# A split-fp32 hybrid trunk on one core: inverse root on ScalarE with a Newton step, x for the value sums on the weights' queue, and a new spread of the block sums

## The chip, the cores and the metric

The kernel runs on one core of one Trainium2 chip. Its time is device microseconds from launch to end; a profile is one further execution of the same program, recorded by the hardware profiler. Engines are named as in the profile: PE (TensorE), with its weight loads as PEld; DVE (VectorE); ACT (ScalarE); POOL (GpSimd); SP (SyncE, here only an issuer of DMAs). "L1704" is line 1704 of the kernel file. Line numbers are those of the kernel before, unless it is said that they belong to the changed one, where the same line stands up to 14 further down.

## The reference

One decoder layer over 512 tokens of width 1024, in fp32:

```
proj  = x @ w_in            # q, k, v of three token mixers, and three gates
o_da  = differential attention (4 heads, two softmax maps, per-head RMSNorm)
o_sb  = stick-breaking attention (8 heads)
o_dl  = dilated windows (3 head groups x 4 heads, outputs of a slot merged
        by their softmax denominators)
m     = (sum_i sigmoid(gate_i) * (o_i @ w_branch_i)) @ w_out
x     = layer_norm(ALPHA * x + m)
x     = layer_norm(ALPHA * x + relu(x @ w_up)**2 @ w_down + gated embedding of p)
```

The per-head RMSNorm of the differential branch is `o * rsqrt(mean(o*o) + eps)`: this is the inverse root that the change computes in another way.

## The kernel before, in words

**Splits.** Every large product is done in three: each fp32 operand is split into a high and a low part, and PE multiplies high with high, high with low, low with high. Weights come in chunks of 128 x 1024 fp32 (512 KB). SP loads a chunk (`fill`, L163 to 186) into a ring of seven; `split_next` (L198 to 219) issues its high part as a cast on ACT (L212, "wh") and its low part as a subtraction on DVE (L214, "wl"), both into rings of six. A cast can run only when PE is done with the tile six chunks back.

**The main stream.** The work is a list of items, each a bank of PSUM filled by a run of matmuls (`mm`) and emptied by an evacuation (`ev`). The main loop (behind L1890) walks the items; between them `step()` advances generators for the attention heads (`sb_head`, `dil_head`, `da_block`) and the forms of x (`value_forms`, `mixer_forms`). A `yield` in a generator says "go on at the next step". So the Python order is an interleaving; a scheduler then fixes each engine's own order when the program is built, and each engine runs its list in that order.

**Seven products and the sums they need.** Many matrix products are done as 2 x 2 blocks with seven products instead of eight. That takes sums of weight blocks and sums of x blocks.
- *Weight sums* are made in DRAM by DMAs that POOL issues: copies (L1046) and accumulating DMAs (L1044), in the order of `sum_steps` (L1017 to 1070). Each has a dependency on `lows[0]`, the weight split four back, so that they spread over the stream. How many go out is a credit: each item adds `size * rate` (L1941 to 1948), and each whole unit issues one step. Late in the kernel the credit is 0.58 an item.
- *x sums for the value projection* (`value_forms`, L343 to 393): eight tiles xr of 128 x 512 fp32 (256 KB each, L347) come by POOL's queue; DVE combines them (L370, L363, L388, tile "fr"), and ACT and DVE split the results (L237 and L238, "u7", "u6", "u4", "u5"). `value_pair` (L395 to 443) uses them for two of the three dilated value groups; its items copy partial results by ACT (L427, L431) and merge them on DVE (L430 to 441, "dl_v"). `load_xr` (L324 to 336, L331) loads x a second time, later, for the gates.

**Around the change in time.** First PE finishes projections of q and k (L87 to 89, evacuated at L285 and L287, "dl_q", "dl_k"). Then the items of `value_pair` (L420 to 422) run, and dilated head 0 beside them: its scores (L1737, L1753 on PE), row maxima on DVE (L1740, L1761), exponentials on ACT (L1746, L1768), the exchange of row statistics between the strided orders by two small matmuls (L1778 with r of L1771, L1780 with r of L1774), a chain of small operations (L1784 to L1800, one exponential on ACT at L1795), the scaling of the tiles (L1802 and L1806 on DVE), transposes on PE (L1821, L1830) and the product with the values (L1842, L1847). Head 0 waits six extra yields ahead of its transposes (L1809).

**The differential branch.** `da_block` (L1649 to 1718) does one head and one quarter of the queries. After the fourth quarter of a head it takes four means of squares "ms" (128 x 4): L1703 on DVE makes mean plus eps, L1704 on POOL raises it to the power -0.5, L1705 on DVE multiplies by the softmax denominators' inverses. On DVE, L1705 holds up what stands behind it. On POOL, L1704 stands among the DMA issues of the weight sums, and an issue waits until one of the eight earlier transfers with its semaphore has landed. Sigmoids of the gates (L501) are issued after the last exponential (`last_exp`), so that ACT changes its function table once.

**The engines' queues.** SP: chunk loads. POOL: weight sums, both loads of x, a few shuffles, L1704.

Of the kernel before, what the change touches and what calls it, by code (L numbers as in the profile page):

```python
# [55 lines left out]
def trunk(tc, a, out):  # L56
    nc = tc.nc
    es = ExitStack()
    with es:
# [76 lines left out]
        ORDERED, AHEAD = 17, 4  # L136
        loads, chunks, placed = [], [], []
        lows = deque(maxlen=4)
        st = {"dma": 0, "split": 0}

        def load(src, w, own=False):
# [56 lines left out]
        def split_next():  # L198
            c = chunks[st["split"]]
            w, off = c["w"], c.get("off", 0)  # L200
            if c.get("pre"):
                c["pre"]()
            if c.get("dst") is None:
                h = ring.tile([P, 1024], F32R, name=nm("wh"), tag="wh", bufs=RING)
                lo = ring.tile([P, 1024], F32R, name=nm("wl"), tag="wl", bufs=RING)
                parts = [(h[:, :w], lo[:, :w], 0, w)]
                c["h"], c["l"] = parts[0][:2]
            else:
                parts = c["dst"]
            for h, lo, a0, a1 in parts:  # L210
                raw = c["from"]["raw"][:, off + a0:off + a1]
                i = nc.scalar.copy(h, raw)  # L212
                st["cast"] = getattr(i, "ins", i)
                i = nc.vector.tensor_sub(lo, raw, h.bitcast(F32))  # L214
                st["low"] = getattr(i, "ins", i)
                lows.append(st["low"])
            for t in (c["from"], *c.get("also", ())):
                t["uses"] -= 1
            st["split"] += 1
# [104 lines left out]
        def load_xr():  # L324

            r = {}
            for h in range(2):
                for th in range(2):
                    for kp in range(2):
                        t = slot("xr")  # L330
                        i = nc.gpsimd.dma_start(t.rearrange("p (k t) -> p k t", k=2),  # L331
                                                xt[:, 4 * h + 2 * kp:4 * h + 2 * kp + 2, 256 * th:256 * th + 256])
                        tc.add_manual_dep(getattr(i, "ins", i), lows[-1].name, mybir.DependencyInfo(
                            mybir.DependencyClass.Sync, mybir.DependencyReason.DATA), reason="not ahead of time")
                        r[h, th, kp] = t
            return [[r[h, th, kp] for kp in range(2)] for h in range(2) for th in range(2)]
# [6 lines left out]
        def value_forms():  # L343

            xr = [slot("xr") for _ in range(8)]
            for k, t in enumerate(xr):
                i = nc.gpsimd.dma_start(t, xt[:, k, :])  # L347
                tc.add_manual_dep(getattr(i, "ins", i), lows[-1].name, mybir.DependencyInfo(
                    mybir.DependencyClass.Sync, mybir.DependencyReason.DATA), reason="not ahead of time")

            def blk(kh, k, th):
                return xr[4 * kh + k].rearrange("p (t c) -> p c t", c=4)[:, 2 * th:2 * th + 2, :]

            def new():
                ts = [slot("fr") for _ in range(2)]
                return ts, [ts[k // 2].rearrange("p (k c t) -> p k c t", k=2, c=2)[:, k % 2] for k in range(4)]

            def parts(p, ts):
                form(vf, p, ts)
                vf[p] = [[(h[:, r * P:r * P + P], lo[:, r * P:r * P + P]) for r in range(2)] for h, lo in vf[p]]  # L360

            def neg_sub(o, i, j):
                nc.vector.scalar_tensor_tensor(o, i, -1.0, j, op0=OP.mult, op1=OP.subtract)  # L363

            for _ in range(WAIT):
                yield
            f7, o7 = new()
            with tc.issue_after(st["low"]):
                for k in range(4):
                    nc.vector.tensor_sub(o7[k], blk(1, k, 1), blk(0, k, 1))  # L370
            parts(7, f7)
            yield
            f6, o6 = new()
            with tc.issue_after(st["low"]):
                for k in range(4):
                    neg_sub(o6[k], o7[k], blk(0, k, 0))
            yield
            parts(6, f6)
            yield
            f4, o4 = new()  # L380
            for k in range(4):
                neg_sub(o4[k], o6[k], blk(1, k, 0))
            yield
            parts(4, f4)
            yield
            f1, o1 = new()
            for k in range(4):
                nc.vector.tensor_sub(o1[k], blk(0, k, 0), blk(0, k, 1))  # L388
            yield
            parts(5, f1)  # L390
            yield
# [53 lines left out]
        def v_items(nv, name, g):  # L445
            cs = [chunk(a["wv"][nv, c].rearrange("p k n -> p (k n)"), 1024) for c in range(4)]
            for tt in range(4):
                def mm(ps, tt=tt):
                    for k in range(8):
                        c = cs[k // 2]  # L450
                        s = slice((k % 2) * 512, (k % 2) * 512 + 512)
                        x1, x2 = xh[k][:, tt * P:tt * P + P], xl[k][:, tt * P:tt * P + P]
                        nc.tensor.matmul(ps, x1, c["h"][:, s], start=k == 0, stop=False)
                        nc.tensor.matmul(ps, x1, c["l"][:, s], start=False, stop=False)
                        nc.tensor.matmul(ps, x2, c["h"][:, s], start=False, stop=k == 7)
                        if k == 3:
                            yield

                def ev(ps, tt=tt):
                    if name == "sb_v":  # L460
                        v = [slot(name, F32R).rearrange("p (h two d) -> p h two d", two=2, d=64) for _ in range(2)]
                        pv = ps.rearrange("p (h d) -> p h d", d=64)
                        for i in range(2):
                            hs = slice(4 * i, 4 * i + 4)
                            nc.scalar.copy(v[i][:, :, 0, :], pv[:, hs, :])
                            nc.vector.tensor_sub(v[i][:, :, 1, :], pv[:, hs, :], v[i][:, :, 0, :].bitcast(F32))
                        V[name, g, tt] = v
                    else:
                        t = slot(name)
                        cp(t, ps)  # L470
                        V[name, g, tt] = t
                item(cs if tt == 3 else [], mm, ev, need=cs)
                items[-1]["rate"] = 1.4

        nt, nv = 2, 0
        order = main_order()
# [62 lines left out]
        def seven(forms, operand, bank_of, done):  # L539

            cs = {}
            for p in (2, 1, 7, 6, 4, 5, 3):
                for r in range(2):
# [19 lines left out]
                    if p == 5:  # L563
                        bank_of.get("sums", set()).add(len(items))
                    item(cs[p] if r else [], mm, ev, need=cs[p], bank=bank, size=0.5)
                    items[-1]["rate"] = 1.2

        msum = [[[dram.tile([P, 1024], F32, name=f"msum{n}_{m}_{i}") for i in range(4)] for m in range(2)]
                for n in range(3)]
# [67 lines left out]
        def branch_items(i):  # L637
            for half in range(2):
                cs = [chunk(a["wb"][i - 1, half, c].rearrange("p k n -> p (k n)"), 1024) for c in range(2)]
                for tt in range(4):  # L640
# [20 lines left out]
                    def pre(tt=tt, half=half):  # L661
                        sg[i, tt, half] = gate_sig(i, tt, half)
                    item(cs if tt == 3 else [], mm, ev, need=cs, bank=None if i == 1 else at_bank, size=0.5)
                    items[-1]["rate"] = 1.5
                    if i != 1:
                        items[-1]["pre"] = pre

# [30 lines left out]
        def branch_seven(i, behind):  # L698

            s, b, cs = {}, {}, {}  # L700
            for p in (2, 1, 7, 6, 4, 5, 3):
                for r in range(2):
# [31 lines left out]
                        m = merged[to]  # L734
                        (nc.vector.tensor_add if p in (1, 3) else nc.vector.tensor_sub)(m, m, g)
                    item([cs[p]] if r else [], mm, ev, need=[cs[p]], bank=bank, size=0.25)
                    items[-1]["rate"] = 1.5
                    to = {2: (r, 0), 7: (r, 1), 6: (2 + r, 1), 4: (2 + r, 0)}.get(p)
                    if to:
                        def pre(to=to):  # L740
# [19 lines left out]
            item([], mm, ev, size=0.08)  # L760

        last_plain = len(items)
        for it in items:
            it.setdefault("rate", 2.6)
        def first_gate(tt, half):
            g = gate_sig(1, tt, half)
            nc.vector.tensor_mul(merged[tt, half], merged[tt, half], g)
# [249 lines left out]
        def sum_steps():  # L1017
# [24 lines left out]
            def issue(o, i, plus):  # L1042
                if plus:
                    i = nc.gpsimd.dma_start(o, i, accum_op=OP.add, max_dma_last_dim=4096)  # L1044
                else:
                    i = nc.gpsimd.dma_start(o, i, max_dma_last_dim=4096)  # L1046

                tc.add_manual_dep(getattr(i, "ins", i), lows[0].name, mybir.DependencyInfo(
                    mybir.DependencyClass.Sync, mybir.DependencyReason.DATA), reason="spread over the main stream")

            w = a["wv"].rearrange("g c p k n -> g c p (k n)")
# [597 lines left out]
        def da_block(hd, qb):  # L1649
# [50 lines left out]
            if da_left[hd] == 0:  # L1700
                yield

                nc.vector.tensor_scalar(ss, ss, 1.0 / P, EPS, op0=OP.mult, op1=OP.add)  # L1703
                nc.gpsimd.tensor_tensor(ss, ss, mhalf.to_broadcast([P, 4]), OP.pow)  # L1704
                nc.vector.tensor_mul(ss, ss, da_rr[hd])  # L1705
                yield
                on = slot("on")
                nc.vector.tensor_mul(on.rearrange("p (b d) -> p b d", b=4), po.rearrange("p (b d) -> p b d", b=4),
                                     ss.unsqueeze(2).to_broadcast([P, 4, P]))
# [11 lines left out]
        def dil_head(hd):  # L1721
            while any(("dl_q", 4 * g + hd) not in T or ("dl_k", 4 * g + hd) not in T for g in range(3)):
                yield

            while hd == 1 and ("dl_v", 1, 3) not in V:
                yield
            q = [T["dl_q", 4 * g + hd] for g in range(3)]
            k = [T["dl_k", 4 * g + hd] for g in range(3)]
# [77 lines left out]
                nc.vector.tensor_scalar(o, o, mxx[:, c:c + 1], None, op0=OP.mult)  # L1806
            yield

            for _ in range(6 if hd == 0 else 0):  # L1809
                yield  # L1810

            src0 = {}
# [89 lines left out]
        for n, it in enumerate(items):  # L1902
# [39 lines left out]
            if 12 <= n < wout_at + 8:  # L1942
                credit += it["size"] * it.get("rate", 1.0)
            elif n > ple_at + 6:
                credit += 0.58
            while credit >= 1:
                credit -= 1
                next(sum_steps_, None)
# [142 lines left out]
```

## Time and profile before

| | us |
|---|---|
| median of 3 runs (lowest to highest) | 1063.72 (1063.63 to 1065.58) |
| the profiled execution | 1063.71 |
| span recorded in it | 1061.8 |
| PE busy / DVE / ACT / POOL in the span | 1039.9 / 773.6 / 589.7 / 182.1 |
| PE idle in the span | 21.9 |
| mean granted clock of PE | 0.991 |

The span is what the profiler saw between the first and the last instruction; 1.9 us of the execution lie around it. In the timelines a row is: start in us, length in us, engine, line, operation, result <- operands, how many, and in brackets how long the engine had been idle and what released it. In the rows of waits the numbers are: us in total, times, the longest. In the groups by line they are: busy us, mean ns of one, idle ahead of them. A matmul's length contains its pipeline, so two neighbours overlap; their distance is the cost. The granted clock is 1.00 when PE may run at full rate.

### The profile page before, as it was taken

How to read it: one execution, taken by the hardware profiler on the slowest of the kernel's cores; microseconds unless marked ns; L12 is line 12 of the kernel's file. 1: busy time of each engine (PE TensorE's matmuls, PEld its weight loads, DVE VectorE, ACT ScalarE, POOL GpSimd, SP SyncE). 2: the span in 40 equal slices, each digit the busy share in tenths (PEclk: the TensorE clock that was granted, in tenths of full speed). 3: DMA queues.
4: the chain of work that ended last, by engine and by line, in shares of the span. 5: the costliest groups of instructions: out<-in, count | busy, mean ns of one | idle time of the engine just before them, and what ended most of it. 6: DMA issues, size and time to landing. Idle time of an engine off the chain costs nothing.

```text
span 1061.8 us, 15061 instructions
## 1 busy us (share of the span) xinstructions
PE 1039.9 (98%) x5462; PEld 884.9 (83%) x5462; DVE 773.6 (73%) x1376; ACT 589.7 (56%) x1002; POOL 182.1 (17%) x279
## 2 busy tenths in 40 slices
PE   9999999998999998999999999999999999999996
PEld 6887788887888886788888888888999989989885
DVE  6887667639864743878766785889677877877966
ACT  6665545526444642667662663685665665666651
POOL 0003303220202312201111122111211111111000
PEclk9999999999999998999999999999999999999998
DMA  8358957995847999637999999179999999999512
GB/s 317 111 169 252 244 160 224 306 280 172 254 133 205 305 284 262 231 103 236 295 295 279 317 311 302 64 254 291 331 333 342 305 275 306 316 284 336 194 38 80
DMA packets 74346, 260.09 MB, mean 245 GB/s; under 512 B 9144, under 2 KB 10056, under 8 KB 74272
## 3 DMA queue, kind: packets, MB, share of 16 engines
q0 software_dynamic: 33616, 120.40, 43.3%
q1 hardware_dynamic: 40080, 137.81, 36.0%
q8 instruction: 43, 0.70, 0.3%
q10 hardware_dynamic: 576, 0.92, 0.2%
q14 instruction: 31, 0.25, 0.1%
HBM read 256.98 MB, written 111.17 MB: 347 GB/s over the span
## 4 chain that ended last, share of the span: by engine, by line
PE 81%; DMA 11%; issue 4%; DVE 2%; ACT 1%; POOL 0%; SPq 0%; DVEq 0%; POOLq 0%; ACTq 0%
PE mm L87 8%; PE mm L88 7%; PE mm L89 7%; DMA msum<-in_wgm_dram 4%; PE at L1207 4%; PE at L1208 4%; PE at L1209 4%; DMA bsum<-bsum 3%; PE at L554 3%; PE at L556 3%; PE at L555 3%; DMA gsum<-in_wg_dram 1%; PE at L89 1%; PE at L88 1%; PE at L87 1%
## 5 line engine op out<-in xcount | busy, mean ns | idle before, releaser
L214 DVE TENSOR_TENSOR wl<-raw,wh 128x1024 fp32r<-128x1024 f32 x254 | 308.9, 1222 | 124.6 <-ACT wh L212 122.4
L212 ACT CAST wh<-raw 128x1024 fp32r<-128x1024 f32 x254 | 265.9, 1050 | 234.6 <-PE mm L88 129.5
L87 PE MATMUL mm<-xhT,wh 128*128 128x512 f32 x304 | 122.6, 403 | 0.0
L89 PE MATMUL mm<-xhT,wl 128*128 128x512 f32 x304 | 120.2, 395 | 0.0
L88 PE MATMUL mm<-xlT,wh 128*128 128x512 f32 x304 | 120.1, 395 | 0.0
L1207 PE MATMUL at<-wh,hh 128*128 128x512 f32 x188 | 73.7, 392 | 0.0
L1208 PE MATMUL at<-wl,hh 128*128 128x512 f32 x188 | 73.7, 392 | 0.0
L87 PE MATMUL mm<-x1hT,wh 128*128 128x256 f32 x256 | 73.7, 288 | 0.0
L1209 PE MATMUL at<-wh,hl 128*128 128x512 f32 x188 | 73.1, 389 | 0.0
L88 PE MATMUL mm<-x1lT,wh 128*128 128x256 f32 x256 | 72.2, 282 | 0.0
L89 PE MATMUL mm<-x1hT,wl 128*128 128x256 f32 x256 | 71.8, 283 | 0.0
L89 PEld LDWEIGHTS mm<-xhT,wl 128*128 128x128 f32 x304 | 58.0, 191 | 12.6
L87 PEld LDWEIGHTS mm<-xhT,wh 128*128 128x128 f32 x304 | 58.0, 191 | 11.8 <-issue 0.4
L88 PEld LDWEIGHTS mm<-xlT,wh 128*128 128x128 f32 x304 | 58.0, 191 | 10.7
L87 PEld LDWEIGHTS mm<-x1hT,wh 128*128 128x128 f32 x256 | 48.7, 190 | 4.7 <-ACT up L1141 2.8
L88 PEld LDWEIGHTS mm<-x1lT,wh 128*128 128x128 f32 x256 | 48.9, 191 | 1.5
L89 PEld LDWEIGHTS mm<-x1hT,wl 128*128 128x128 f32 x256 | 48.6, 191 | 0.0
L1044 POOL DMA_DIRECT2D usum<-in_wu_dram x32 | 27.0, 871 | 112.9 <-DVE wl L214 84.2
L1209 PEld LDWEIGHTS at<-wh,hl 128*128 128x128 f32 x188 | 35.3, 188 | 7.7
L1044 POOL DMA_DIRECT2D dsum<-in_wd_dram x28 | 24.0, 878 | 101.9 <-DVE wl L214 68.0
L1207 PEld LDWEIGHTS at<-wh,hh 128*128 128x128 f32 x188 | 35.5, 189 | 6.0
L1208 PEld LDWEIGHTS at<-wl,hh 128*128 128x128 f32 x188 | 35.5, 189 | 5.5
(604 smaller groups left out, 2675.0 us busy)
## 6 DMA issues: line engine op xcount, KB each, us to landing
usum<-in_wu_dram POOLq DMA_DIRECT2D x48, 512.0 KB, 8.6
dsum<-in_wd_dram POOLq DMA_DIRECT2D x42, 512.0 KB, 8.5
raw<-in_wt_dram SPq DMA_DIRECT2D x38, 512.0 KB, 6.0
msum<-in_wgm_dram POOLq DMA_DIRECT2D x36, 512.0 KB, 14.3
raw<-usum SPq DMA_DIRECT2D x32, 512.0 KB, 7.4
raw<-dsum SPq DMA_DIRECT2D x28, 512.0 KB, 7.5
raw<-in_wd_dram SPq DMA_DIRECT2D x25, 512.0 KB, 6.1
raw<-msum SPq DMA_DIRECT2D x24, 512.0 KB, 7.6
```

What stands on the lines that cost most here:

```text
L87: nc.tensor.matmul(ps, wh, xh, start=start, stop=False, skip_group_check=True)
L88: nc.tensor.matmul(ps, wh, xl, start=False, stop=False, skip_group_check=True)
L89: nc.tensor.matmul(ps, wl, xh, start=False, stop=stop, skip_group_check=True)
L212: i = nc.scalar.copy(h, raw)
L214: i = nc.vector.tensor_sub(lo, raw, h.bitcast(F32))
L554: nc.tensor.matmul(ps, h[:, q], c["h"][:, n], start=go, stop=False, skip_group_check=True)
L555: nc.tensor.matmul(ps, h[:, q], c["l"][:, n], start=False, stop=False, skip_group_check=True)
L556: nc.tensor.matmul(ps, lo[:, q], c["h"][:, n], start=False, stop=end, skip_group_check=True)
L1044: i = nc.gpsimd.dma_start(o, i, accum_op=OP.add, max_dma_last_dim=4096)
L1207: nc.tensor.matmul(ps, h[:, q], c["h"][:, s], start=go, stop=False, skip_group_check=True)
L1208: nc.tensor.matmul(ps, h[:, q], c["l"][:, s], start=False, stop=False, skip_group_check=True)
L1209: nc.tensor.matmul(ps, lo[:, q], c["h"][:, s], start=False, stop=end, skip_group_check=True)
```

## The change

Five edits in one.

1. The inverse root leaves POOL. ACT takes the logarithm and the exponential of minus half of it (y), DVE adds one Newton step, `y * (1.5 - 0.5 * s * y * y)`, in three operations; there is a `yield` ahead of them. The exponential counts as the last one for the sigmoids.
2. The loads of x in `load_xr` and `value_forms`, 16 DMAs, go from POOL's queue to SP's.
3. `marks` replaces `lows` for the weight sums: it holds the same splits, and each evacuation of a plain value item twice. Those evacuations are now all on DVE; before, they alternated between ACT and DVE (`cp`).
4. Rates of the credit change: 1.4 to 2.5 for plain value items, 1.2 to 1.4 in `seven`, 1.5 to 1.4 in `branch_items` and `branch_seven`, and the two below.
5. Dilated head 0 waits until the forms of product 5, the last ones, are issued (`5 not in vf`), and then two extra yields instead of six.

In the built program PE's instructions are the same 5241. POOL has 20 rows fewer and SP 16 more, DVE 16 more and ACT 4 more. PE's order differs around `value_pair`: L1737 of head 0 comes after three value items (it came ahead of all of them), L1753 after that, and L1778 after five more items; elsewhere it has three small swaps. In the order of DVE the maxima of head 0 now stand behind the forms of products 7, 6, 4 and 5 and the splits among them.

```diff
+        marks = deque(maxlen=4)
...
                 lows.append(st["low"])
+                marks.append(st["low"])
...
-                        i = nc.gpsimd.dma_start(t.rearrange("p (k t) -> p k t", k=2),
+                        i = nc.sync.dma_start(t.rearrange("p (k t) -> p k t", k=2),
                                                 xt[:, 4 * h + 2 * kp:4 * h + 2 * kp + 2, 256 * th:256 * th + 256])
...
-                i = nc.gpsimd.dma_start(t, xt[:, k, :])
+                i = nc.sync.dma_start(t, xt[:, k, :])
...
-                        cp(t, ps)
+                        i = nc.vector.tensor_copy(t, ps)
+                        marks.append(getattr(i, "ins", i))
+                        marks.append(getattr(i, "ins", i))
...
-                items[-1]["rate"] = 1.4
+                items[-1]["rate"] = 2.5
...
-                    items[-1]["rate"] = 1.2
+                    items[-1]["rate"] = 1.4
...
-                    items[-1]["rate"] = 1.5
+                    items[-1]["rate"] = 1.4
...
-        for it in items:
-            it.setdefault("rate", 2.6)
+        for j, it in enumerate(items):
+            it.setdefault("rate", 2.5 if j < 45 else 1.9)
...
-                tc.add_manual_dep(getattr(i, "ins", i), lows[0].name, mybir.DependencyInfo(
+                tc.add_manual_dep(getattr(i, "ins", i), marks[0].name, mybir.DependencyInfo(
...
                 nc.vector.tensor_scalar(ss, ss, 1.0 / P, EPS, op0=OP.mult, op1=OP.add)
-                nc.gpsimd.tensor_tensor(ss, ss, mhalf.to_broadcast([P, 4]), OP.pow)
+                y = small("ir", 4)
+                nc.scalar.activation(y, ss, AF.Ln)
+                e = nc.scalar.activation(y, y, AF.Exp, scale=-0.5)
+                last_exp[0] = getattr(e, "ins", e)
+                yield
+                nc.vector.scalar_tensor_tensor(ss, ss, -0.5, y, op0=OP.mult, op1=OP.mult)
+                nc.vector.tensor_mul(ss, ss, y)
+                nc.vector.scalar_tensor_tensor(ss, ss, 1.5, y, op0=OP.add, op1=OP.mult)
                 nc.vector.tensor_mul(ss, ss, da_rr[hd])
-                yield
...
             while hd == 1 and ("dl_v", 1, 3) not in V:
+                yield
+            while hd == 0 and 5 not in vf:
                 yield
...
-            for _ in range(6 if hd == 0 else 0):
+            for _ in range(2 if hd == 0 else 0):
                 yield
...
             elif n > ple_at + 6:
-                credit += 0.58
+                credit += 0.6
```

More of the change, by code (lines that the diff above doesn't have):

```diff
@@ L736, in branch_seven @@
                     item([cs[p]] if r else [], mm, ev, need=[cs[p]], bank=bank, size=0.25)
-                    items[-1]["rate"] = 1.5
+                    items[-1]["rate"] = 1.4
                     to = {2: (r, 0), 7: (r, 1), 6: (2 + r, 1), 4: (2 + r, 0)}.get(p)
```

## The prediction

> **What bounds the kernel now.** I read the waits of TensorE first, then the windows, then the timelines around the two longest waits, and the groups and DMA rows of those stretches last.
>
> ```profile
> span 1061.8 us, 15061 instructions
> PE 1039.9 (98%) x5462; PEld 884.9 (83%) x5462; DVE 773.6 (73%) x1376; ACT 589.7 (56%) x1002; POOL 182.1 (17%) x279
> ...
> PE at L1778 <- DVE r L1771: 4.1, 1, 4.1
> PE mm L420 <- ACT dl_q L285: 3.6, 1, 3.6
> ...
> PE mm L647 <- DVE da_klb L101: 1.1, 1, 1.1
> PE at L1780 <- DVE r L1774: 1.1, 1, 1.1
> ```
>
> PE is the bound: it is idle for 1061.8 - 1039.9 = 21.9 us, and half of that is start and tail, which the change leaves alone. Four waits in the middle, 4.1 + 3.6 + 1.1 + 1.1 = 9.9 us, can be won, and what they cost in granted clock.
>
> ```profile
> 240.20:250.00 9.80, 8.00 (x35) 7.34 (x36) 8.38 (x18) 3.91 (x6) 0.00 (x0) 0.83 0.46 163
> 255.40:268.80 13.40, 13.40 (x61) 11.10 (x61) 13.40 (x36) 10.99 (x23) 1.03 (x2) 1.00 0.70 235
> 287.00:400.00 113.00, 112.67 (x601) 95.69 (x600) 67.61 (x218) 51.94 (x126) 22.57 (x33) 1.00 0.83 237
> 400.00:425.00 25.00, 19.81 (x80) 15.73 (x79) 9.10 (x41) 7.23 (x21) 7.03 (x10) 0.80 1.03 262
> ```
>
> Columns: window, length, busy PE, weight loads, DVE, ACT, POOL, then clock, DMA share, GB/s. The clock is below 1.00 only behind the two long waits. And in 255.4 to 268.8 DVE is busy for 13.40 of 13.40 us beside a full PE: whatever more has to come early on DVE there makes PE wait.
>
> **First wait: x for the value sums.** PE needs the bank that ACT frees with dl_q (L285), which stands behind casts of forms that DVE makes (L370) from x.
>
> ```profile
> 213.73 6.50 SPq L182 DMA_DIRECT2D raw<-in_wv_dram  x2
> ...
> 214.00 1.26 POOL L347 DMA_DIRECT2D xr<-in_xT_dram  x2 [3.64 <-DVE wl L214]
> ...
> 233.24 0.54 POOL L347 DMA_DIRECT2D xr<-in_xT_dram  x1 [3.03 <-DMA msum<-in_wgm_dram]
> ...
> 236.69 1.17 DVE L370 TENSOR_TENSOR fr<-xr,xr 128x256 f32<-128x256 f32 x2 [9.91 <-PE mm L88]
> 236.69 1.68 PE L1737 MATMUL at<-dl_k,dl_q 128*128 128x128 f32 x8
> 240.29 1.04 ACT L212 CAST wh<-raw 128x1024 fp32r<-128x1024 f32 x1
> 241.35 0.60 ACT L285 ACTIVATE dl_q<-mm 128x512 f32<-128x512 f32 x1
> 242.00 0.62 PE L420 MATMUL mm<-wh,xhT 128*128 128x512 f32 x1 [3.63 <-ACT dl_q L285]
> 242.93 0.40 PE L420 MATMUL mm<-wh,xhT 128*128 128x512 f32 x1
> 243.17 0.40 PE L421 MATMUL mm<-wl,xhT 128*128 128x512 f32 x1
> 243.79 0.63 PE L420 MATMUL mm<-wh,xhT 128*128 128x512 f32 x1
> 246.35 2.19 PE L1753 MATMUL at<-dl_k,dl_q 128*128 128x128 f32 x16
> ```
>
> POOL issues the eight loads one by one from 214.0 to 233.2 behind accumulates that occupy its queue; the last lands near 238.5 (233.24 and some 5 us), where DVE's last L370 can begin. Soon after the wait matmuls last 0.63 us, not 0.40, and stand 0.2 further apart: seven of them lose 1.4 us, and L1753 about 1.0, half of its 2.19.
>
> **Second wait: the inverse root.**
>
> ```profile
> 409.66 1.32 POOL L1704 TENSOR_TENSOR ms<-ms,mhalf 128x4 f32<-128x4 f32 x1
> ...
> 400.99 0.17 DVE L1744 TENSOR_SCALAR nm<-st 128x4 f32<-128x4 f32 x1
> 411.02 0.16 DVE L1705 TENSOR_TENSOR ms<-ms,rr 128x4 f32<-128x4 f32 x1 [9.87 <-POOL ms L1704]
> 411.10 0.18 DVE L1771 TENSOR_TENSOR r<-st,exf 128x32 f32<-128x32 f32 x1
> ...
> 411.43 0.60 PE L1778 MATMUL at<-r,fold 128*128 128x32 f32 x2 [4.14 <-DVE r L1771]
> ...
> ...
> 420.67 0.52 PE L88 MATMUL mm<-xlT,wh 128*128 128x512 f32 x1
> ```
>
> POOL raises to the power only after DMA issues, each of which waits for a landing. DVE stands at L1705 for 9.87 us, and r (L1771), behind it in DVE's order, lets PE wait.
>
> **The change, part by part.**
>
> *Root on ACT with a Newton step.* In the changed order of DVE r stands ahead of the three new operations and needs only ACT's four exponentials behind nm (there at 401.2), some 2 us: it is ready near 403.3, 4 us before PE arrives (411.43 - 4.14 = 407.3). The 4.14 us go, the 1.05 behind them too, and the slow clock: from 411.85 to 420.7, less the 1.1 of waiting and L1780 itself, 17 matmuls at 0.427 instead of 0.227, 3.4 us. What is late next is r of the second half: its maxima and four exponentials follow on 403.3 and end near 408.8 by the order, where PE arrives: an estimate of 0.3 us left. Gain 4.1 + 1.1 + 3.4 - 0.3 = **8.3 us**. The price is four times two small ACT and three DVE operations (like L1705, 0.16 us), beside PE: nothing as long as ACT is half idle. A change of its function table would cost ACT 1.3 us a time (below), but the changed program holds three loads as before; were each root to bring two, 2.6 us on ACT would still fit into the 4 us ahead of PE.
>
> ```profile
> L501 ACT ACT_TABLE_LOAD x1 | 1.3, 1283 | 0.0
> ```
>
> *The wait at L647 (1.1 us)* goes by order: DVE now makes da_klb ahead of a weight split. Gain **1.1 us**; with neither, 0.
>
> *x on SP's queue.* All eight follow the weight chunk that SP issues at 213.73; the last must wait for that chunk's landing (some 8 us). Queued behind them is only the next chunk, whose split comes 30 us later: free. The sums' accumulates stay on the other queue, so the two share the DMA engines:
>
> ```profile
> q0 software_dynamic: 129, 0.46, 66.3%
> q1 hardware_dynamic: 121, 0.50, 37.1%
> ...
> raw<-in_wv_dram SPq DMA_DIRECT2D x1, 512.0 KB, 7.8
> ...
> q1 hardware_dynamic: 88, 0.36, 24.2%
> ```
>
> In 217.0 to 220.5 SP's queue moved 0.50 MB in 3.5 us, 143 GB/s, half of the packets. The 2.10 MB of x behind a chunk that lands at 221.5 take 14.7 us: last landing **236**. Ends: 90 GB/s (182 to 186, the last row, 0.36 MB in 4 us) gives 245; the whole 282 GB/s or so that both queues move gives 229. I take 236, the row in the very place. The pages differ from this: the Trainium skill, "DMA: Bandwidth & Descriptors", section "Issuing engines are not separate DMA queues", holds that a second issuing engine saves only issue time, which would leave the landing at 238.5. The row of half shares speaks for a gain of turn, because here x stood behind accumulates of its own queue; the rule is a rival below.
>
> From the last landing to dl_q it was 242.0 - 238.5 = 3.5 us, of which 0.5 was DVE finishing earlier L370; 3.0 remain, dl_q is done at 239.0. PE arrives at 236.7, since the order now puts L1737's 1.7 us later: it waits **2.3 us** instead of 3.63, and by the rows (1.1 us left the clock full, 3.63 halved it) keeps its clock: the 2.4 us are saved.
>
> *Head 0 of the dilated branch waits for the forms.* Its maxima (L1740, L1761) now follow on DVE the forms for all products and six splits; before, they stood ahead. From the first split whose ACT cast waits for PE (the seventh matmul of one product item) to the first scaling L1802 that PE's transposes L1821 need, DVE has in the changed order: six L214, four L388, three L238, seven additions like L430, all maxima, some 16 small operations.
>
> ```profile
> L214 DVE TENSOR_TENSOR wl<-raw,wh 128x1024 fp32r<-128x1024 f32 x6 | 7.3, 1214 | 1.1 <-ACT wh L212 1.1
> L388 DVE TENSOR_TENSOR fr<-xr 128x256 f32<-128x256 f32 x4 | 2.4, 629 | 0.0
> ...
> L1740 DVE CUSTOM_DVE_ANT_0 L<-at,shf 128x256 f32<-128x256 f32 (+1 forms) x4 | 1.3, 381 | 0.0
> L1761 DVE CUSTOM_DVE_ANT_0 L<-at,shf,ma 128x128 f32<-128x128 f32 x4 | 1.3, 355 | 0.0
> ...
> L1761 DVE CUSTOM_DVE_ANT_0 L<-at,shf 128x128 f32<-128x128 f32 x4 | 1.0, 296 | 0.0
> L238 DVE TENSOR_TENSOR u5l<-fr,u5h 128x512 fp32r<-128x512 f32 x1 | 0.7, 696 | 0.0
> ...
> L430 DVE TENSOR_TENSOR dl_v<-dl_v,mm 128x512 f32<-128x512 f32 x1 | 0.7, 676 | 0.0
> ```
>
> That is 7.3 + 2.4 + 3 x 0.7 + 7 x 0.68 + 3.6 + 1.1 for reading the maxima + 16 x 0.17 = 24.0 us. Each starts 0.08 us before the one ahead ends (411.02 + 0.16 against 411.10): 59 of them make 4.7 less, 19.3; waits for ACT's casts and exponentials in the order add about 1.7: 21 us, and the cast ahead (1.04) 22.1. PE meanwhile has 5 + 60 matmuls at 0.235 (242.93 to 243.17) and 0.5 us of small ones, 15.8. So PE waits 22.1 - 15.8 = **6.3 us**, in parts of about 0.9, 0.9 and 4.5, the last at L1821. An earlier x does not help: the cast waits for PE. Ends: 2 us, if I miscount the order's waits and overlap; 9, if DVE's early part is late as well. The 4.5 us wait is above 3.63 and halves the clock: 2.4 to 3.4 us, I take **2.4**.
>
> By its rule, in "TensorE: Matmul & The Clock Gate", Part 1, the Trainium skill ties the half clock to an idle window of about 3.4 us that runs freely; a wait of 4.5 us need not fill one. Both waits above that length did cost clock here (3.63 and 4.14); the rule makes the other outcome a rival.
>
> *Rates, marks, evictions on DVE.* Sums go out a few us earlier, none later than its reader by the distances of before (10 us and more). Four evictions of 0.68 us move to DVE at places where PE waits for nothing. Cost 0, ends -1 and +2, in case the transfers crowd a chunk: the window 287 to 400 with its 112.67 of 113.00 has no such wait at 237 GB/s.
>
> **Sum.** Stage 236 to 287: before, 3.63 + 2.4 = 6.0 us lost; after, 2.3 + 6.3 + 2.4 = 11.0: +5.0. With -8.3 and -1.1 the sum is -4.4. The profiled execution took 1063.71 us (span 1061.8), at the median of 1063.72, so the forecast is **1059.3**.
>
> **Rivals.**
> - *DVE keeps up* (the maxima fit between the splits). For: windows count overlap. Against: 13.40 of 13.40. Stage: 2.3 against 6.0: 1063.7 - 9.4 - 3.7 = 1050.6.
> - *The 4.5 us wait costs no clock*: 1059.3 - 2.4 = 1056.9.
> - *x lands no earlier* (238.5): PE waits 4.8 us at L420 and pays for two slow clocks. 4.8 + 2.4 + 6.3 + 2.4 = 15.9 against 6.0: 1063.7 - 9.4 + 9.9 = 1064.2, no change. This is what the rule on issuing engines comes to.
> - *Slower: x loses its turn on SP's queue.* At 90 GB/s it lands at 245, PE waits 11.3 us at L420: 1064.2 + 6.5 = 1070.7. It decides from a landing after 240.2 on (1065.9). For: single chunks came at 90 beside accumulates. Against: 143 in the place itself, and eight loads queue without gaps.
>
> **How the numbers follow.** A measurement tells 0.2%, about 2.1 us, from no change. Forecast 0.46, clock kept 0.12, DVE keeps up 0.10, all faster: 0.68. x no earlier 0.17: same. Slower 0.15. The range leaves out the best and the worst case, and takes x from 230 to 240: 1052 to 1066.
>
> **What would show it.** Right: no 9.87 us idle on DVE near 401, PE at L1778 without a wait at 407; xr on SP's queue, last landing about 236; PE waiting at L1821 behind DVE's scaling, near 270, and a clock below 1 there. Wrong: windows 250 to 275 with full PE, or a wait at L420 over 3.4 us.

## The result and the profile after

The changed kernel takes 1067.07 us (median of 18 runs, 1065.44 to 1068.65), the kernel before beside it 1064.96 (18 runs, 1062.60 to 1067.38). The ratio is 1.0020, 95% interval 1.0012 to 1.0027: **slower by 2.1 us**, where 1059.3 was forecast, and outside the range. The gain that was forecast did come; more than it went into the stage of the value products. The profiled execution of the changed kernel took 1068.65 us, 1.6 above the median, so its rows need not fit the medians to better than that. One run of e6 took 5.7 ms and is left out of e6's ratio and median.

The waits of PE in the changed kernel (us in total, times, longest). Line numbers are those of the changed file: L422 was L420, L1790 was L1778, L1833 was L1821.

```profile
PE mm L422 <- ACT dl_q L287: 8.4, 1, 8.4
PE at L1833 <- DVE L L1814: 4.9, 1, 4.9
PE at L1389 <- DVE zero L1386: 1.3, 1, 1.3
PE at L1790 <- DVE r L1783: 1.1, 1, 1.1
...
PE mm L422 <- ACT dl_v L429: 0.4, 1, 0.4
```

The 4.1 us of the inverse root and the 1.1 us at the branch product are gone, and the row at L1790 now belongs to head 0. The wait for dl_q has grown from 3.6 to 8.4 us, and 4.9 us stand at the transposes of head 0. The windows of the same kernel (length, busy PE, weight loads, DVE, ACT, POOL, clock, DMA share, GB/s):

```profile
236.70:250.00 13.30, 4.86 (x15) 3.66 (x14) 8.40 (x13) 3.95 (x7) 0.00 (x0) 0.68 0.70 226
250.00:275.00 25.00, 24.64 (x112) 21.71 (x111) 19.22 (x46) 13.11 (x23) 1.63 (x2) 0.97 0.53 154
275.00:300.00 25.00, 19.01 (x84) 15.84 (x83) 18.53 (x44) 10.72 (x22) 4.07 (x7) 0.86 0.56 148
...
400.00:425.00 25.00, 25.00 (x136) 21.53 (x134) 11.29 (x45) 11.17 (x34) 3.72 (x6) 1.00 0.74 215
```

400 to 425, in which both kernels have the exchange of row statistics behind the inverse root (L1778 at 411.4 before, L1790 at 422.4 now), went from 19.81 busy at a clock of 0.80 to a full 25.00 at 1.00. Before 300 there are now two stretches with a poor PE and a low clock, where there was one. The second lies behind the wait at L1833, where six matmuls cost some 0.43 us each and not 0.23:

```profile
285.10 1.73 PE L1833 MATMUL at<-ident,L 128*128 128x128 f32 x7 [4.92 <-DVE L L1814]
286.48 0.78 PE L422 MATMUL at<-wh,u4h 128*128 128x512 f32 x1
287.05 0.63 PE L423 MATMUL at<-wl,u4h 128*128 128x512 f32 x1
...
288.76 0.59 PE L424 MATMUL at<-wh,u4l 128*128 128x512 f32 x1
289.18 0.39 PE L422 MATMUL at<-wh,u4h 128*128 128x512 f32 x1
```

Why dl_q is late is seen on DVE, where the first forms (L372, L370 before) wait for x piece by piece:

```profile
237.30 0.61 DVE L372 TENSOR_TENSOR fr<-xr,xr 128x256 f32<-128x256 f32 x1 [9.18 <-DMA xr<-in_xT_dram]
239.22 0.61 DVE L372 TENSOR_TENSOR fr<-xr,xr 128x256 f32<-128x256 f32 x1 [1.31 <-DMA xr<-in_xT_dram]
...
243.75 0.61 DVE L372 TENSOR_TENSOR fr<-xr,xr 128x256 f32<-128x256 f32 x1 [2.52 <-DMA xr<-in_xT_dram]
```

The last piece lands at 243.7, not at 236. And this is what the two queues moved from 222 to 228, when SP's (q1) had hardly anything but x at work and POOL's (q0) weight sums; the columns are packets, MB, time that the packets took as a share of 16 engines' span. The row of the issue has KB and us to landing; it is the last load of x, issued at 223.6, when the chunk ahead of x had landed:

```profile
q0 software_dynamic: 272, 0.98, 82.0%
q1 hardware_dynamic: 269, 0.50, 25.0%
...
xr<-in_xT_dram SPq DMA_DIRECT2D x1, 256.0 KB, 20.1
```

The numbers of packets are equal, 272 and 269. The bytes are not: 0.50 MB in 269 packets is 1.9 KB each, 0.98 MB in 272 is 3.6 KB (the rows are of 2 and 4 KB; a few packets are under 512 B). x moves at 84 GB/s. In the window that I took my 143 GB/s from, a chunk of weights was in SP's queue: 121 packets for 0.50 MB, 4.1 KB each.

84 GB/s is not the rate of all of x. From 228 to 236 the counts are equal again, and both queues move faster:

```profile
q0 software_dynamic: 519, 1.89, 69.5%
q1 hardware_dynamic: 520, 0.94, 33.6%
```

That is 117 GB/s for x. By these rows a packet of the sums took 0.29 us of an engine before 228 and 0.17 us behind it. Over the 20.1 us from the chunk's landing to its own last one, x comes to 104 GB/s.

### The profile page after: what moved, and what is told of

Read it like the earlier page. It is cut to its first block, busy times and chain, and to the rows that moved or that the text cites. A ratio compares the mean times of both kernels' runs of the same rounds, so it can differ in the third digit from the quotient of the medians.

```text
span 1066.9 us, 15075 instructions
## 1 busy us (share of the span) xinstructions
PE 1039.9 (97%) x5462; PEld 883.7 (83%) x5462; DVE 778.8 (73%) x1392; ACT 589.7 (55%) x1006; POOL 167.5 (16%) x259
## 4 chain that ended last, share of the span: by engine, by line
PE 88%; DVE 4%; DMA 3%; ACT 2%; issue 2%; SPq 0%; POOL 0%; DVEq 0%; POOLq 0%
PE mm L87 9%; PE mm L89 9%; PE mm L88 9%; PE at L1211 4%; PE at L1212 4%; PE at L1213 4%; PE at L558 3%; PE at L560 3%; PE at L559 3%; PE mm L455 2%; PE mm L457 2%; PE mm L456 2%; DMA xr<-in_xT_dram 2%; PE at L89 1%; PE at L88 1%
## 5 line engine op out<-in xcount | busy, mean ns | idle before, releaser
L215 DVE TENSOR_TENSOR wl<-raw,wh 128x1024 fp32r<-128x1024 f32 x254 | 309.1, 1222 | 127.7 <-ACT wh L213 125.5
L88 PEld LDWEIGHTS mm<-xlT,wh 128*128 128x128 f32 x304 | 57.2, 188 | 10.6
L1048 POOL DMA_DIRECT2D msum<-in_wgm_dram x24 | 21.3, 927 | 126.1 <-DVE wl L215 61.6
```

What stands on the lines that cost most here:

```text
L88: nc.tensor.matmul(ps, wh, xl, start=False, stop=False, skip_group_check=True)
```

## The experiments

All ratios are against the kernel before, run beside them. Where two changed kernels are compared below, the difference is that of their medians; by the ratios, which share the noise of the kernel before, it comes out up to 1.7 us different.

| kernel | us | ratio (95% interval) |
|---|---|---|
| e1 root alone | 1055.24 | 0.9907 (0.9891 to 0.9922) |
| e9 marks, evictions and rates alone | 1055.33 | 0.9911 (0.9893 to 0.9929) |
| e7 x on SP alone | 1066.54 | 1.0010 (0.9998 to 1.0022) |
| e6 wait of head 0 alone | some 1075.9 | 1.0099 (1.0077 to 1.0122) |
| e2 all but x on SP | 1065.99 | 1.0006 (0.9997 to 1.0015) |
| e3 all but the wait of head 0 | 1056.44 | 0.9923 (0.9903 to 0.9944) |
| e4 all, x in 4 KB rows | 1064.16 | 0.9988 (0.9977 to 0.9999) |
| e5 all, sums in 2 KB packets | 1063.32 | 0.9969 (0.9952 to 0.9986) |
| e8 root, fewer sums ahead of x | 1049.11 | 0.9840 (0.9826 to 0.9855) |
| e10 e8 and the wait of head 0 | 1058.42 | 0.9943 (0.9926 to 0.9961) |
| e11 e8 and the second x on SP | 1048.39 | 0.9844 (0.9829 to 0.9860) |

The theory to begin with: the root gives all of the gain; head 0's wait and the late x take it back; x is late because packets of the two queues alternate one for one, and x's rows of 512 fp32 make 2 KB packets beside the sums' 4 KB. The main rivals: x is late because of its place behind a chunk on SP, or because of the new spread of the sums; the waits of head 0 only follow from the late x.

### e1: the root alone

```diff
-                nc.gpsimd.tensor_tensor(ss, ss, mhalf.to_broadcast([P, 4]), OP.pow)
+                y = small("ir", 4)
+                nc.scalar.activation(y, ss, AF.Ln)
+                e = nc.scalar.activation(y, y, AF.Exp, scale=-0.5)
...
```

> The kernel before with edit 1 alone (logarithm, exponential and Newton step instead of POOL's power). My account of the changed kernel gives this edit all of the gain: the 4.1 us wait at L1778, the 1.1 us at L1780 and 3.4 us of half clock behind them go, and with them perhaps the 1.1 us at L647: 8 to 10 us faster than before, 0.991 of its time. The rival, that the root's gain was partly due to the other edits' timing, expects less than 5 us.

1055.24, 9.9 us faster by the ratio. Its waits of PE:

```profile
PE mm L420 <- ACT dl_q L285: 3.9, 1, 3.9
PE at L1385 <- DVE zero L1382: 1.3, 1, 1.3
PE mm L647 <- DVE da_klb L101: 1.1, 1, 1.1
```

The rows of L1778 and L1780 are gone, and nothing else is. The stall with its clock was worth 8.6 us by the prediction's rows (4.1 + 1.1 + 3.4); where the other 1.3 us come from was not followed up. It does not touch the 1.1 us at L647.

### e9: marks, evictions and rates alone

```diff
-                        cp(t, ps)
+                        i = nc.vector.tensor_copy(t, ps)
+                        marks.append(getattr(i, "ins", i))
...
-            it.setdefault("rate", 2.6)
+            it.setdefault("rate", 2.5 if j < 45 else 1.9)
...
```

> The kernel before with edits 3 and 4 alone (marks, evictions of value items on DVE, rates). I costed them at 0, ends -1 and +2. The kernel with all edits but x's queue had x landing near 241 on POOL's queue, 2 us later than before: if the new spread does that, this kernel waits 5 to 6 us for dl_q instead of 3.6 and is 1 to 3 us slower; otherwise within 1 us.

1055.33: neither. I had costed these edits at nothing, and alone they are worth as much as the root. POOL's instructions around the second root (L1704, here L1708) in this kernel:

```profile
401.42 0.52 POOL L1050 DMA_DIRECT2D gsum<-gsum  x1 [5.49 <-DVE wl L215]
402.53 1.04 POOL L1708 TENSOR_TENSOR ms<-ms,mhalf 128x4 f32<-128x4 f32 x1 [0.60 <-DVE ms L1707]
403.54 0.58 POOL L1050 DMA_DIRECT2D usum<-usum  x1
```

The power still runs on POOL, but at 402.5 and not at 409.7: the weight sums are further ahead, so the issues beside it wait for a split (L215) and not for landings. Root and rates remove the same stall; their gains don't add: both together, on top of head 0's wait, gave 9.9 us (e2 against e6, by the ratios), as the root does alone. In return x waits for more: PE's wait for dl_q rose to 4.9 us here (3.9 in e1).

### e6 and e3: head 0 waits for the forms, added alone and taken out

```diff
+            while hd == 0 and 5 not in vf:
+                yield
...
-            for _ in range(6 if hd == 0 else 0):
+            for _ in range(2 if hd == 0 else 0):
```

> The kernel before with edit 5 alone (head 0 waits for the forms, two yields). If it is this edit that ate the gain, it costs what its removal from the changed kernel gave: 8 to 11 us slower than before, with waits at the two small matmuls and the transposes of head 0 of about 6 us in all, and L1737's 1.7 us taken out of the time before the wait for dl_q. The rival, that it only costs together with the late x, expects under 4 us.

> The changed kernel without edit 5 (dilated head 0 does not wait for the forms, six yields as before). If head 0's maxima behind the forms cost 6.4 us of waits and 2.4 us of half clock, this is 7 to 9 us faster than the changed kernel, with the wait for dl_q still at 7 to 9 us. If the waits at L1790 and L1833 only follow from the late x, they stay, at L1790 and L1833 or elsewhere in 250 to 290, and the gain is under 3 us.

Alone it makes the kernel before take 1.0099 times as long, 10.5 us more; taken out of the changed kernel it gives 10.6 (1067.07 to 1056.44). The us of e6 in the table are the median of three runs. The waits of e6, where L1780 and L1823 are the first small matmul and the transposes:

```profile
PE at L1780 <- DVE r L1773: 6.0, 2, 5.0
PE mm L420 <- ACT dl_q L285: 5.3, 1, 5.3
PE at L1823 <- DVE L L1804: 5.1, 2, 4.9
```

The 5.0 us at L1780 are the root's stall, here as before. The other two rows are the edit: 1.0 and 4.9 us behind DVE's forms, and a wait for dl_q of 5.3 instead of 3.6, since L1737's 1.7 us no longer fill it. Taken out (e3), the waits behind DVE vanish:

```profile
PE mm L422 <- ACT dl_q L287: 6.2, 1, 6.2
PE at L1389 <- DVE zero L1386: 1.3, 1, 1.3
PE at L131 <- ACT da_ka L122: 0.8, 2, 0.6
```

So the rival, that these waits only follow from a late x, is out; e10 says it once more from the other side.

### e7 and e2: x on SP's queue, added alone and taken out

```diff
-                i = nc.gpsimd.dma_start(t, xt[:, k, :])
+                i = nc.sync.dma_start(t, xt[:, k, :])
...
```

> The kernel before with edit 2 alone (both loads of x on SP's queue). By packet shares x at 84 GB/s needs some 25 us behind the chunk, against about 24 us on POOL's queue from 214 to 238.5: lands at 240 to 244, and the wait for dl_q grows from 3.6 to 5 to 8 us: 1 to 4 us slower than before. My forecast's step (x at half of the bytes, landing at 236) would make it 3 to 5 us faster.

> The changed kernel with both loads of x back on POOL's queue. If x is late because its 2 KB packets on SP's queue alternate one for one with the sums' 4 KB packets, it lands near 239 again instead of 243.7, PE waits about 4 us for dl_q instead of 8.4, the waits of 6.4 us behind DVE stay: 3 to 5 us faster than the changed kernel. If x is late because of the sums' new spread (more accumulates ahead of it), it stays late also here: within 1.5 us of the changed kernel, or slower.

Alone 1.0 us slower (the interval reaches to no change), taken out 1.1 us faster (1.5 by the ratios): a small loss. The wait for dl_q is 6.5 us in e7 against 3.6, and 6.9 us in e2 against 8.4. That is less than the packet theory expected of e2, and half of the spread's rival is right: in e2 x stays late, the last form starting at 241.2, and POOL issues the last load at 236.0 instead of 233.2. One way to build the wait of 8.4 us from single profiles is 3.6 before, 1.7 for L1737 (e6), 1.6 for the spread (e2 against e6), 1.5 for SP's queue (the changed kernel against e2). Another is 3.6, 2.9 for SP's queue (e7) and 1.7 for L1737, which leaves next to nothing for the spread; and e3, with the spread and x on SP's queue, waits 6.2 us, no more than e7. So the spread delays x only on POOL's queue, behind the sums; in the changed kernel it is SP's queue that makes x late. Part of the 2.9 us that e7 loses at dl_q is given back: the kernels with both loads of x on SP lack the 1.1 us at L647 (see e11).

### e5: the sums in packets of 2 KB

```diff
-                    i = nc.gpsimd.dma_start(o, i, accum_op=OP.add, max_dma_last_dim=4096)
+                    i = nc.gpsimd.dma_start(o, i, accum_op=OP.add, max_dma_last_dim=2048)
...
```

> The changed kernel with the packets of the weight sums at 2 KB instead of 4 KB; x stays on SP's queue with its 2 KB packets. If packets of the two queues alternate one for one, x moves half of the bytes beside the sums instead of a third: some 120 to 140 GB/s instead of 84, lands 4 to 7 us earlier than 243.7, and the wait for dl_q falls from 8.4 us to 2 to 4 us. If the share of x has nothing to do with packet sizes, landing and wait stay within 1.5 us. Small packets may slow the sums themselves; later readers have room.

The queues of e5 from 222 to 228:

```profile
q0 software_dynamic: 421, 0.81, 72.5%
q1 hardware_dynamic: 415, 0.75, 38.3%
```

Again as many packets in one queue as in the other, 421 and 415, and now as many bytes: x moves at 125 GB/s, its last form starts at 238.0 instead of 243.7, and PE waits 3.8 us instead of 8.4. The last load takes 17.1 us behind the chunk instead of 20.1, and the chunk itself, in 4 KB packets beside 2 KB ones, 6.8 us instead of 8.5: together 4.7 us. Nothing of x, its queue or its place had changed. The kernel is 3.7 us faster than the changed one (1063.32 to 1067.07; 5.4 by the ratios). This is the run that settles that the packets' sizes made x late on SP's queue. They are not all of it: with equal packets x still needs 17.1 us, where 14.7 were forecast.

### e4: x in rows of 4 KB

```diff
-            xr = [slot("xr") for _ in range(8)]
+            x2 = [ring.tile([P, 1024], F32, name=nm("xr"), tag="raw", bufs=RAW) for _ in range(4)]
...
```

> The changed kernel with the eight loads of x for the value forms made as four of twice the size, so that a row is 4 KB instead of 2 KB (into the ring of weight chunks); same queue, same place behind the same chunk. Packet theory: x moves at about 139 GB/s beside the sums instead of 84, lands near 236 to 238, and the wait for dl_q falls from 8.4 us to 2 to 4 us, 5 to 8 us faster than the changed kernel (with the half clock). Queue theory (x is late because it stands behind a chunk and its issues are held back on SP): landing and wait stay within 1.5 us of 243.7 and 8.4.

PE's wait fell to 3.3 us, but this run tells less than it was made for. The four wide tiles had to go into the ring of weight chunks, and SP could issue them only as its buffers came free:

```profile
220.51 22.14 SPq L351 DMA_DIRECT2D xr<-in_xT_dram  x4
...
246.18 1.13 DVE L374 TENSOR_TENSOR fr<-xr,xr 128x256 f32<-128x256 f32 x2 [3.89 <-DMA xr<-in_xT_dram]
...
248.63 0.62 PE L424 MATMUL mm<-wh,xhT 128*128 128x512 f32 x1 [3.34 <-ACT dl_q L287]
```

From 220.5 to 242.3 instead of from 215 to 223. So x was later here, not earlier: its last forms start at 246.2 (243.7 in the changed kernel), and PE gets dl_q at 248.6 (246.6 there). The wait is short because in this kernel's order PE has value items and head 0's first scores to do ahead of it. The landing that the packet theory expected, 236 to 238, was missed, and the wait of 2 to 4 us came for another reason. What bears on the theory is the stretch from 224 to 226, when one of the wide loads was under way beside the sums:

```profile
q0 software_dynamic: 71, 0.26, 64.6%
q1 hardware_dynamic: 73, 0.30, 39.1%
```

As many packets in one queue as in the other once more, now with 4.1 KB each in SP's: x moves at some 150 GB/s while it moves. The 4.9 us at the transposes stayed.

### e8: fewer sums ahead of x

```diff
-                credit += it["size"] * it.get("rate", 1.0)
+                rate = it.get("rate", 1.0)
+                if v_from[0] - 7 <= n < v_from[0]:
+                    rate = 0.8
+                elif v_from[0] - 14 <= n < v_from[0] - 7 or 0 <= n - v_from[0] < 14:
+                    rate += 1.0
+                credit += it["size"] * rate
```

> The kernel before with edit 1, x on POOL's queue, and the credit of the sums moved: 2 or 1 more an item in the seven items from 14 to 8 ahead of the value forms and in 14 items behind their start, 0.8 in the seven items between, so that fewer sums stand ahead of x. If the wait for dl_q is bought by the sums ahead of x, x lands before 233, the wait of 3.9 us and its half clock go: 5 to 7 us faster than edit 1 alone (1055.2), about 1049. If x is bound by something else, no gain over edit 1 alone.

With the root on ACT, x on POOL's queue, and this: 1049.11, 6.1 us below e1, which has the root alone. The longest waits of its PE but that of the start; the others are of 0.2 us:

```profile
PE mm L647 <- DVE da_klb L101: 1.1, 1, 1.1
PE at L131 <- ACT da_ka L122: 0.8, 2, 0.6
PE at L131 <- ACT da_kb L124: 0.3, 1, 0.3
```

x's last form starts near 231.6, before PE needs it. On POOL's queue it was the sums ahead of x that held it up, and the place to mend it is their schedule. That fewer sums would help x on SP's queue too is to be expected from e5, but was not run.

### e10: the early x with head 0's wait

> The kernel with edit 1 and the early x (1049.1) plus edit 5: head 0 waits for the forms, while x is early. My account says that the stretch on DVE cannot be helped by an earlier x, since a weight cast in it waits for PE: waits of 6 us at the small matmuls and the transposes stay and the time is 6 to 10 us longer than 1049.1. The rival, that edit 5 was meant for an early x and costs nothing then, expects under 2 us.

1058.42, 9.3 us slower than e8 (11 by the ratios), with x's forms begun at 230.2. Its waits:

```profile
PE at L1829 <- DVE L L1810: 5.1, 2, 4.9
PE at L1385 <- DVE zero L1382: 1.3, 1, 1.3
PE mm L647 <- DVE da_klb L101: 1.1, 1, 1.1
PE at L1786 <- DVE r L1779: 1.1, 1, 1.1
```

The same 4.9 and 1.1 us as with the late x: the stretch of DVE is anchored to PE, not to x.

### e11: the second load of x on SP's queue

```diff
-                        i = nc.gpsimd.dma_start(t.rearrange("p (k t) -> p k t", k=2),
+                        i = nc.sync.dma_start(t.rearrange("p (k t) -> p k t", k=2),
```

> The kernel with edit 1 and the early x (1049.1) plus the second load of x alone (for the gates) on SP's queue. All four kernels with x on SP so far have no wait at the branch product behind da_klb, all others have 1.1 us there: if it is this load that orders DVE's work so, the wait goes and the time is about 1 us less, 1048. If it was the first load or chance, no change.

1048.39; PE's wait at L647 is gone from its list. So it is this load's queue that removes the wait. What that is worth in time is not shown: the median is 0.7 us below that of e8, but the ratios to the kernel before, run beside each, are 0.9844 and 0.9840. How the load's queue changes DVE's order there was not followed up. e8 and e11 are the fastest versions that were run, 1.6% below the kernel before.

## Why the prediction was wrong, point by point

- **Root on ACT: right.** Forecast 8.3 us with the clock; 400 to 425 is full, and alone the edit gives 9.9. That another edit of the same change would have given this gain too (e9) was not seen: I priced the rates by transfers that crowd each other, not by POOL's instruction that stands among the issues.
- **The wait at L647: right, it is gone** (1.1 us). The prediction named the order on DVE and not what changes it; it is the queue of the second load of x (e11).
- **Head 0's wait: right.** Forecast 6.3 us in parts of 0.9, 0.9 and 4.5; measured 0.4 + 1.1 + 4.9 = 6.4. That the sum came out to 0.1 us is in part luck. That an earlier x does not help was right (e10). The half clock behind L1833 came as well: six matmuls at 0.43 us and slow transposes cost some 1.9 us, forecast 2.4. The rival that charged no clock is refuted here: the waits of 3.3 us and more that were looked at were all followed by matmuls at half rate, and a wait of 1.1 us left a full clock full. The Trainium skill, "TensorE: Matmul & The Clock Gate", Part 1, with its window of about 3.4 us that runs freely, lets a wait of 4.5 us go free or not; no run here shows one that went free, and the 3.3 us of e4, a little under that window, cost clock too.
- **x on SP's queue: here it failed.** The step was "143 GB/s, half of the packets ... 2.10 MB take 14.7 us: last landing 236". Half of the packets was right; that half of the packets is half of the bytes was not. I had read a row in which both queues carried 4 KB packets, and put a load with 2 KB rows in its place. x moved at 84 GB/s at first and at 104 in the mean, instead of 143: 20.1 us instead of 14.7, a last landing at 243.7 instead of 236, a wait of 8.4 us instead of 2.3, and the half clock behind it, 12 matmuls and 2.4 us, which I had saved. By e5, 3.0 of the 5.4 us between 14.7 and 20.1 are the packets' size; the other 2.4 were not taken apart.
- **What that step cost.** The stage lost 8.4 + 6.4 + 2.4 + 1.9 = 19.1 us where 11.0 were forecast. Of the 8.1 us between them, 6.1 + 2.4 are this step, and 0.4 the other way are head 0's. With the root's 9.9 for 8.3, the forecast's -4.4 becomes -4.4 - 1.6 + 8.1 = +2.1, as measured, which is closer than single profiles can promise.
- My slower rival had nearly the right rate, x at 90 GB/s, for another reason (that it runs beside accumulates), and too small a chance. Its row does not show that rate either: in 182 to 184 SP's queue had little to move (20 packets beside 98), and from 184 to 186 it moved 68 beside 66.
- The rule of the Trainium skill that I weighed against the step, "DMA: Bandwidth & Descriptors", section "Issuing engines are not separate DMA queues", came out right: a second issuing engine bought no bandwidth. From 222 to 228 both queues together moved 246 GB/s in e7 and 251 before, and e7 was not faster. The rival that I hung on it, a landing at 238.5, was too early all the same.
- **Rates: wrong as a cost of 0.** They have two effects of their own: alone a gain of 9.5 us by the ratio, by freeing POOL for the root, which edit 1 hides here; and a later x as long as x is on POOL's queue (a wait of 4.9 us in e9 for 3.6). Neither stood in my sum, and in the changed kernel neither shows.

The single edits add up once the double gain is counted once: -9.9 (e1) + 10.5 (e6) + 1.0 (e7) = +1.6, and 2.1 was measured.

## What to carry to other kernels

When a transfer is moved to another queue, its share of the DMA engines goes by packets as long as both queues are busy: look at the row length of what is moved and of what it will run beside, and multiply. When an edit delays an engine's work behind other work of the same engine, add up that engine's durations over the stretch against the bound engine's; here it gave the waits within 0.5 us each. And ask of every edit that is priced at nothing whether it removes the same stall as another one.

## What the runs showed of the hardware that I had not expected

- Two DMA queues that are both busy alternate one packet each, whatever the size: 272 to 269 packets with 3.6 and 1.9 KB each, 421 to 415 with equal ones, 71 to 73 in e4 with 4 KB ones. The Trainium skill, "DMA: Bandwidth & Descriptors", section "Queues, rings and completion order", has the engines go round the queues packet by packet; the counts agree, with a "packet" of the profile as the unit.
- The same load makes other packets on another queue: the two loads of x, moved from POOL to SP, raise the packets of the whole execution from 74346 to 76394.
- Behind every wait of PE for dl_q of 3.3 us or more that was looked at (3.3 in e4, 3.8 in e5, 4.9 in e9, 6.9 in e2, 8.4 in the changed kernel), 6 to 12 matmuls ran at half rate, which costs some 1.3 to 2.4 us beside the wait; behind the 4.1 us of the inverse root it was 17, and behind a wait of 1.1 us with a full clock none. The number did not grow with the wait.
